# The kernel's last waits, for its stores, moved from SyncE to ScalarE and put in the order of the stores

## The chip, the cores and the metric

The kernel runs on one core of a Trainium2 chip. The metric is the device time of one execution in microseconds (us). The core has five instruction streams that run side by side and meet through semaphores: TensorE (PE, with its weight loads as PEld), VectorE (DVE), ScalarE (ACT), GpSimd (POOL) and SyncE (SP), which computes nothing here and issues transfers.

## The reference

```python
def setup_inputs():
    batch, seq, hidden, n_heads = (16, 512, 768, 12)
...
    y = np.matmul(x, weight)
    y = y.reshape(batch, seq, n_heads, head_dim)
    y1, y2 = (y[..., :head_dim // 2].copy(), y[..., head_dim // 2:].copy())
...
    out1 = y1 * cos1 - y2 * sin1
    out2 = y2 * cos2 + y1 * sin2
    out = np.concatenate([out1, out2], axis=-1)
    return out.reshape(batch, seq, hidden).astype(np.float32)
```

A projection of 16 x 512 rows by a 768 x 768 weight, and then the rotation of each of the 12 heads of 64 columns by cosines and sines that depend on the row. `x` and the result are float32, 25.17 MB each.

## The kernel before

The 8,192 rows are cut into 64 tiles of 128 rows, and four tiles make a group, so there are 16 groups; `LAST` is 15. A tile's rows are loaded as float32, cast to float16, turned so that the contracted dimension lies on the partitions, and multiplied by the weight into PSUM (`py`, in the last group also `pt`). VectorE multiplies PSUM by cosines and sines at once (line 412, into `tq`), and an addition, nearly always on GpSimd (line 429), puts the two products together into one of four output buffers `ov0` to `ov3`, each of which holds a group (128 x 3072 float32). `store` (line 453) issues a transfer of a part of such a buffer to the output, from the queue of the engine that is named to it: ScalarE (`"act"`) or SyncE (`"sp"`).

The order of the work is written out by hand. `Flow.do` records each instruction on its engine in the order of the calls and works out, from what was read and written before, which semaphores it waits for. Every store has a semaphore of its own, named for buffer and first column, `ov3_2560` for one; a store's landing adds 16 to it. Transfers are not ordered among themselves by anything else, so the program has to wait for the stores before it ends. `Flow.finish` (line 95) does that: it collects what wrote or read the named columns, drops what is already known to be past, and makes its engine wait for the rest. In this kernel thirteen semaphores remain: two for each of `ov0`, `ov1` and `ov2`, and seven for the pieces of the last group in `ov3`.

The last group's stores are issued in small pieces, since its sums come ready late: columns 0 to 768 from SyncE, 768 to 1536 from ScalarE, 1536 to 2048 from SyncE, 2048 to 2304 from ScalarE, 2304 to 2560 from SyncE, 2560 to 2816 from ScalarE and 2816 to 3072 from SyncE. The sum for the last of these is made by VectorE (`late`), those before it by GpSimd. `nc.gpsimd.drain()` at line 678 stands behind GpSimd's last addition.

In the built program, the waits of `finish` stand two to an instruction: six semaphore instructions on SyncE (line 102), and the thirteenth wait on the branch that leaves the kernel's body (line 116). The pairs, in the program's order, are 3_768 and 3_0, 3_1536 and 2_1536, 3_2048 and 2_0, 3_2304 and 1_1536, 3_2560 and 1_0, 3_2816 and 0_1536, and 0_0 on the branch. Then comes a closing sequence that the compiler adds. SyncE sets a semaphore, called the exit flag here. Each of the five engines has an instruction (a drain, on GpSimd a no-op) that waits for the exit flag and then reports. SyncE waits for the reports: one instruction for those of VectorE and TensorE, one for its own and ScalarE's, one for GpSimd's. After that, two barriers over all engines, with GpSimd in the middle and a clearing of semaphores between them, end the program (line 717).

Of the kernel before, what the change touches and what calls it, by code (L numbers as in the profile page):

```python
# [16 lines left out]
class Flow:  # L17
# [8 lines left out]
    def __init__(self, nc, tc):  # L26
        self.nc, self.tc = nc, tc
        self.eng = {
            "pe": nc.tensor, "dve": nc.vector, "act": nc.scalar,
            "pool": nc.gpsimd, "sp": nc.sync,  # L30
        }
        self.sems, self.count, self.known = {}, {}, {}
        self.wrote, self.readby = {}, {}
        self.seen = {e: {} for e in self.eng}

# [6 lines left out]
    def do(self, e, make, reads=(), writes=(), dma=None, tick=True, after=0):  # L42
        need = {}
        for k in reads:
            for s, v in self.wrote.get(k, {}).items():
                need[s] = max(need.get(s, 0), v)
        for k in writes:
            for d in (self.wrote, self.readby):
                for s, v in d.get(k, {}).items():
                    need[s] = max(need.get(s, 0), v)  # L50
        if e == "pe":
            need.pop("pe", None)
            if after:
                need["pe"] = after
        waits = self.settle(e, need)
        for s, v in waits[:-1]:
            self.eng[e].wait_ge(self.sem(s), v)
        i = make(self.eng[e])
        if waits:
            s, v = waits[-1]  # L60
            i.wait_op(self.sem(s), v, "sem-ge")
        name, step = (dma, 16) if dma else (e, 1)
        self.sem(name)
        at = self.count[name] + step
        if tick or dma:
            i.then_inc(self.sems[name], step)
            self.count[name] = at
            self.known[name, at] = dict(self.seen[e])
        for k in reads:
            d = self.readby.setdefault(k, {})  # L70
            d[name] = max(d.get(name, 0), at)
        for k in writes:
            self.wrote[k] = {name: at}
            self.readby[k] = {}
        return i
# [19 lines left out]
    def finish(self, e, keys):  # L95
        need = {}
        for k in keys:
            for d in (self.wrote, self.readby):
                for s, v in d.get(k, {}).items():
                    need[s] = max(need.get(s, 0), v)  # L100
        for s, v in self.settle(e, need):
            self.eng[e].wait_ge(self.sem(s), v)


# [1 line left out]
def kernel(  # L106
# [11 lines left out]
    f = Flow(nc, tc)  # L118
# [3 lines left out]
    B, S, H = x.shape  # L122
# [7 lines left out]
    QB = 4  # L130
# [3 lines left out]
    LAST = NG - 1  # L134
# [9 lines left out]
    NX, NB, NBH, NC, NCP, NXT, NXP, NOV = 10, 3, 3, 5, 2, 8, 4, 4  # L144
# [43 lines left out]
    def where(i):  # L188
        g, s = divmod(i, QB)
        return QB * (g // SB) + s, g % SB  # L190
# [10 lines left out]
    def load(i, e="sp"):  # L201
        b, r = where(i)
        k = ring("xs", NX)
        xs[i] = k
        do(e, lambda eng: eng.dma_start(  # L205
            out=xs_b[k], in_=x[b].rearrange("(p r) h -> r p h", r=SB)[r]),
            writes=[f"xs{k}"], dma=f"xs{k}")

    def load_quarter(gh, q):
        g, h = gh  # L210
        b, r = where(g * QB + 2 * h)
        e = BLOCKS[gh]
        src = x[b : b + 2].rearrange("b (j a r) (q k) -> r q a (b j) k", r=SB, a=R, q=NQ)
        if q == 0:
            xs[gh] = ring("xh", NBH) if e == "pool" else ring("xb", NB)
        k = xs[gh]
        name = f"xh{k}" if e == "pool" else f"xb{k}"
        buf = xh_b[k] if e == "pool" else xb_b[k]
        dst = buf.rearrange("p (j k) -> p j k", j=2 * NQ)
        do(e, lambda eng: eng.dma_start(out=dst[ts(q, R)], in_=src[r, q]),  # L220
           writes=[f"{name}q{q}"], dma=name)
# [3 lines left out]
    def load_w(c, e="sp"):  # L225
        t, h = c
        do(e, lambda eng: eng.dma_start(out=w_raw[:, t, h], in_=wv[t, h]),  # L227
           writes=[f"wr{t}{h}"], dma=f"w{t}{h}")
# [214 lines left out]
    def store(g, c0, c1, e):  # L443

        o = ov_of[g]
        b, r = where(g * QB)
        s0, s1 = c0 // H, -(-c1 // H)
        dst = out.rearrange("b (p r) h -> r p b h", r=SB)[r, :, b + s0 : b + s1]
        src = ov_b[o].rearrange("p (b h) -> p b h", b=QB)[:, s0:s1]
        if (c1 - c0) % H:  # L450
            dst = dst[:, 0, c0 - s0 * H : c1 - s0 * H]
            src = src[:, 0, c0 - s0 * H : c1 - s0 * H]
        do(e, lambda eng: eng.dma_start(out=dst, in_=src),
           reads=[f"ov{o}c{c}" for c in range(c0, c1, 64)], dma=f"ov{o}_{c0}")
# [153 lines left out]
    for g in range(LAST):  # L608
        for h in (0, 2):
            i = QB * (g + 1) + h  # L610
            q = (g, h * H, (h + 2) * H, "act")
# [6 lines left out]
            else:  # L618
                q = q[:3] + ("sp",)
# [22 lines left out]
    for i in range(QB, NTILE):  # L642
        g, s = divmod(i, QB)
# [35 lines left out]
    store(LAST, 2 * H, 2048, "sp")  # L679
    store(LAST, 2048, 3 * H, "act")  # L680
    store(LAST, 3 * H, 3 * H + 256, "sp")
    store(LAST, 3 * H + 256, 3 * H + 512, "act")
    for add in late:
        add()
    store(LAST, 3 * H + 512, 4 * H, "sp")
    f.finish("sp", [f"ov{o}c{c}" for o in range(NOV) for c in range(0, QB * H, 64)])


# [33 lines left out]
```

## Time and profile before

| | us |
|---|---|
| time before, median of 3 runs | 151.16 |
| the three runs | 151.91, 151.16, 151.03 |
| the profiled execution, its own time | 151.57 |
| its span, first to last instruction | 149.8 |
| lies around the span | 1.8 |
| PE busy | 141.1 (94%) |
| DVE busy | 126.4 (84%) |
| POOL busy | 122.9 (82%) |
| ACT busy | 78.0 (52%) |

TensorE is busy nearly throughout, until the last slices, in which the work runs off through VectorE, GpSimd and the stores. The mean granted TensorE clock is 0.989 of full speed. Starts are counted from the first instruction of the span. The views of the profile round starts to 0.1 us; where a text gives a start to the nanosecond, it is the start of the same record in the trace.

### The profile page before, as it was taken

To read this page: it belongs to the slowest core of one execution; us is meant where nothing else is said; L and a number is where in the kernel's file an instruction comes from. 1 tells how busy PE (TensorE), PEld (TensorE's weight loads), DVE (VectorE), ACT (ScalarE), POOL (GpSimd) and SP (SyncE) were. 2 spreads that over 40 slices of the span, in tenths; PEclk is the share of its full clock that TensorE was granted. 3 is DMA by queue.
4 is the path that set the end of the run, shared out by engine and by line. 5 is a ranking of instruction groups with operands and counts; after the bars stand their busy time and mean duration, and the time that the engine had idled before them with its cause. 6 is when DMAs were issued, how large, how long until landed. Compare 5 with 4: busy or idle time off the path is not lost.

```text
span 149.8 us, 4360 instructions
## 1 busy us (share of the span) xinstructions
PE 141.1 (94%) x1926; PEld 112.4 (75%) x1926; DVE 126.4 (84%) x92; ACT 78.0 (52%) x92; POOL 122.9 (82%) x68
## 2 busy tenths in 40 slices
PE   6969999999999999999999999999999999999940
PEld 2435578888888888888888888888888888856520
DVE  0154999887888899899999998999989998999980
ACT  3444798787777934456262905283336826163000
POOL 1000396999989998999999999999995979999990
PEclk9999999999999999999999999999999999999995
DMA  4999999999999999999999999999999999966683
GB/s 113 382 376 402 405 400 396 306 405 264 295 371 343 343 355 360 298 402 328 356 345 391 361 334 357 363 392 319 357 363 410 415 404 402 388 272 231 263 315 108
DMA packets 27555, 51.27 MB, mean 342 GB/s; under 512 B 7184, under 2 KB 13072, under 8 KB 27536
## 3 DMA queue, kind: packets, MB, share of 16 engines
q1 hardware_dynamic: 14592, 27.92, 53.9%
q10 hardware_dynamic: 7504, 21.10, 35.6%
q0 software_dynamic: 5440, 1.97, 10.7%
q8 instruction: 15, 0.25, 0.6%
q14 instruction: 4, 0.03, 0.1%
HBM read 27.79 MB, written 25.17 MB: 354 GB/s over the span
## 4 chain that ended last, share of the span: by engine, by line
PE 80%; DVE 6%; DMA 5%; POOL 3%; issue 2%; SPq 1%; POOLq 0%
PE py L360 70%; DMA w_raw<-in_weight_dram 5%; PE py L335 4%; PE pt L266 4%; POOL ov L429 3%; DVE w_raw L412 2%; DVE tq L412 2%; SPq L205 1%; PE pt L251 1%; DVE ov L429 1%; SPq L227 1%; POOLq L678 0%; DVE w_sb L185 0%; SPq L717 0%; SPq L116 0%
## 5 line engine op out<-in xcount | busy, mean ns | idle before, releaser
L429 POOL TENSOR_TENSOR ov<-tq 128x1536 f32<-128x1536 f32 (+3 forms) x31 | 77.5, 2520 | 19.4 <-DVE tq L412 19.3
L360 PE MATMUL py<-w_sb,xt 64*128 64x512 f16 (+1 forms) x864 | 81.4, 323 | 0.0
L412 DVE TENSOR_TENSOR tq<-py,csn 128x1024 f32<-128x1024 f32 (+2 forms) x46 | 74.6, 1652 | 5.2 <-PE py L360 4.9
L360 PEld LDWEIGHTS py<-w_sb,xt 64*128 64x128 f16 x864 | 61.0, 94 | 10.1 <-DVE tq L412 0.4
L185 ACT COPY xt<-pt 128x768 f16<-128x768 f16 x42 | 33.5, 800 | 45.7 <-PE pt L266 44.5
L185 ACT CAST xc<-xs 128x768 f16<-128x768 f32 x44 | 39.1, 907 | 13.9 <-DMA xs<-in_x_dram 13.7
L360 PE MATMUL py<-w_sb,xp 64*128 64x512 f16 (+1 forms) x432 | 42.6, 323 | 0.0
L412 DVE TENSOR_TENSOR w_raw<-py,csn 128x1024 f32<-128x1024 f32 (+1 forms) x21 | 35.2, 1674 | 3.7 <-PE py L360 3.5
L429 POOL TENSOR_TENSOR ov<-w_raw 128x1536 f32<-128x1536 f32 (+1 forms) x11 | 33.7, 3070 | 3.2 <-DVE w_raw L412 2.9
L360 PEld LDWEIGHTS py<-w_sb,xp 64*128 64x128 f16 x432 | 31.1, 94 | 4.7
L335 PE MATMUL py<-w_sb,xt 128*128 128x256 f16 (+1 forms) x90 | 15.7, 323 | 1.3 <-DVE w_sb L185 1.1
L266 PEld LDWEIGHTS pt<-ident,xc 64*128 64x128 f16 x456 | 14.8, 95 | 1.7 <-ACT xc L185 0.6
L266 PE MATMUL pt<-ident,xc 64*128 64x64 f16 x456 | 15.0, 190 | 0.0
L335 PEld LDWEIGHTS py<-w_sb,xt 128*128 128x128 f16 x90 | 8.1, 98 | 7.0 <-DVE w_sb L185 2.7
L220 POOL DMA_DIRECT2D xh<-in_x_dram x20 | 11.7, 590 | 0.0
L185 ACT CAST xd<-xb 128x1536 f16<-128x1536 f32 x5 | 8.2, 1636 | 0.2 <-DMA xb<-in_x_dram 0.2
L514 PE MATMUL py<-cold 128*128 128x512 f16 x12 | 5.0, 584 | 1.4 <-DVE cold L457 1.4
L185 DVE CAST w_sb<-w_raw 128x768 f16<-128x768 f32 x6 | 3.3, 558 | 3.4 <-DMA w_raw<-in_weight_dram 3.4
L294 DVE STREAM_TRANSPOSE xp<-xh 128x768 f32<-128x768 f32 x5 | 6.2, 1231 | 0.0
L185 DVE COPY xt<-pt 128x768 f16<-128x768 f16 x2 | 1.1, 558 | 5.5 <-PE pt L251 5.5
L294 DVE STREAM_TRANSPOSE xp<-xd 128x768 f32<-128x768 f32 x5 | 4.8, 969 | 0.0
L335 PE MATMUL py<-w_sb,xp 128*128 128x512 f16 (+1 forms) x24 | 4.2, 327 | 0.0
(20 smaller groups left out, 18.0 us busy)
## 6 DMA issues: line engine op xcount, KB each, us to landing
out_dram<-ov ACTq DMA_DIRECT2D x26, 768.0 KB, 8.6
xs<-in_x_dram SPq DMA_DIRECT2D x44, 384.0 KB, 17.7
xb<-in_x_dram SPq DMA_DIRECT2D x20, 192.0 KB, 17.4
out_dram<-ov SPq DMA_DIRECT2D x4, 768.0 KB, 4.7
w_raw<-in_weight_dram SPq DMA_DIRECT2D x6, 384.0 KB, 7.3
xh<-in_x_dram POOLq DMA_DIRECT2D x20, 96.0 KB, 12.9
out_dram<-ov SPq DMA_DIRECT2D x1, 384.0 KB, 2.6
out_dram<-ov ACTq DMA_DIRECT2D x1, 384.0 KB, 2.3
```

The costliest lines, as they stand in the source:

```text
L185: eng.copy(out=o, in_=i_) if e == "act" else eng.tensor_copy(out=o, in_=i_)
L205: do(e, lambda eng: eng.dma_start(out=xs_b[k], in_=x[b].rearrange("(p r) h -> r p h", r=SB)[r]), writes=[f"xs{k}"], dma=f"xs{k}")
L220: do(e, lambda eng: eng.dma_start(out=dst[ts(q, R)], in_=src[r, q]), writes=[f"{name}q{q}"], dma=name)
L227: do(e, lambda eng: eng.dma_start(out=w_raw[:, t, h], in_=wv[t, h]), writes=[f"wr{t}{h}"], dma=f"w{t}{h}")
L251: do("pe", lambda eng: eng.transpose(pt[:, t, h, :], src[:, t, h, :], ident), reads=[f"xc{c}", "ident"], writes=[f"pt{k}"], tick=(t, h) == ...
L266: do("pe", lambda eng: eng.transpose(pts[r][:, t, h, :], src[rows, t, h, :], ident[rows, rows]), reads=[f"xc{c}", "ident"], writes=[f"pt{r ...
L294: do("dve", lambda eng: eng.transpose(out=dst, in_=src), reads=rd, writes=[f"xp{z}"])
L335: do("pe", lambda eng: eng.matmul(ps, get(t, h), w_sb[:, t, h, a - s * H : z - s * H], start=start, stop=stop), reads=[key, f"w{t}{h}"], w ...
L360: do("pe", lambda eng: eng.matmul(py[:, a:z], get(t, h)[rows], w_sb[rows, t, h, a - s * H : z - s * H], start=start, stop=not opens and en ...
L412: do("dve", lambda eng: eng.tensor_tensor(out=tq.rearrange("p j (h d) -> p j h d", d=D), in0=ps.rearrange("p (h d) -> p h d", d=D) .unsque ...
L429: do(adder, lambda eng: eng.tensor_tensor(out=ov_b[o][:, ds(c0, w)].rearrange("p (h t d) -> p h t d", t=2, d=HD), in0=tq[:, 0].rearrange(" ...
L514: do("pe", lambda eng: eng.matmul(py[:, ts(b, 512)], cold[:, 0:P], cold, start=True, stop=warmed[0] < WARM - 6), reads=["cold"], writes=[f ...
```

## The change

`finish` is called for ScalarE in place of SyncE. Its waits are reduced to those for the stores' semaphores (names that begin with `ov`), sorted by the time at which they were last used, newest first, and handed out in a zigzag. `do` keeps, for each semaphore, a number that grows with every use, to sort by. The call that issues ScalarE's last store, of columns 2560 to 2816, is moved down behind SyncE's last one; each engine's own order of stores stays what it was.

```diff
-        self.sems, self.count, self.known = {}, {}, {}
+        self.sems, self.count, self.known, self.order = {}, {}, {}, {}
...
         self.sem(name)
+        self.order[name] = len(self.order) + sum(self.count.values())
         at = self.count[name] + step
...
-        for s, v in self.settle(e, need):
+        need = {s: v for s, v in need.items() if s.startswith("ov")}
+        old = sorted(self.settle(e, need), key=lambda q: -self.order[q[0]])
+        for s, v in old[:1] + old[1::2] + old[2::2][::-1]:
             self.eng[e].wait_ge(self.sem(s), v)
...
     store(LAST, 3 * H, 3 * H + 256, "sp")
-    store(LAST, 3 * H + 256, 3 * H + 512, "act")
     for add in late:
         add()
     store(LAST, 3 * H + 512, 4 * H, "sp")
-    f.finish("sp", [f"ov{o}c{c}" for o in range(NOV) for c in range(0, QB * H, 64)])
+    store(LAST, 3 * H + 256, 3 * H + 512, "act")
+    f.finish("act", [f"ov{o}c{c}" for o in range(NOV) for c in range(0, QB * H, 64)])
```

In the built program, the zigzag comes out as pairs from the oldest store to the newest: 0_0 and 0_1536, 1_0 and 1_1536, 2_0 and 2_1536, 3_0 and 3_768, 3_1536 and 3_2048, 3_2304 and 3_2816, all on ScalarE, and 3_2560 on ScalarE's branch. SyncE's branch waits for nothing. The closing sequence is the same, instruction for instruction: SyncE sets the exit flag, every engine reports behind it, and SyncE gathers the reports. On PE, DVE and POOL the program is unchanged apart from line numbers, and so is everything ahead of the last waits on SP and ACT.

## The prediction

> **What bounds the kernel now.** I read the chain of waits first. Most of it is matmul, which this change leaves as it is, so only its end matters. Asked for the stretch from 140 us on, in order of time (start, length, what), it closes like this:
>
> ```profile
> 142.80 1.96 POOL ov L429 x2
> 144.76 0.68 POOLq L678
> 145.44 0.86 POOL ov L429
> ```
>
> The last computing instruction, GpSimd's sum for columns 2560 to 2816, ends at 145.44 + 0.86 = 146.30 us. The span ends at 149.8, so 3.5 us lie behind it, and only there can the edit act. Next I read the transfers issued between 146.2 and 146.9 us and SyncE's waits from 146 us on (total, times, longest):
>
> ```profile
> out_dram<-ov ACTq DMA_DIRECT2D x1, 128.0 KB, 1.8
> ```
>
> ```profile
> SPq L102 <- DMA out_dram<-ov: 1.5, 2, 0.9
> ```
>
> ScalarE's last store is issued at 146.337 and needs 1.8 us to land; SyncE stands in line 102 for it, 0.9 us in the longest wait. The trace has the last update of that store's semaphore at 148.113, and the last of SyncE's own last store (columns 2816 on) at 147.762: ScalarE's is the store that ends last. So from 148.113 on, what counts is how many steps lie between this landing and the end. For these I read the instructions of line 102 and of line 116, engine by engine (count, durations in ns, first and last start):
>
> ```profile
> L102 SPq EVENT_SEMAPHORE  x6: 28/28/28, 146.4 to 148.2; - x6
> ```
>
> ```profile
> L116 SPq EVENT_SEMAPHORE  x3: 17/27/28, 148.4 to 148.7; - x3
> L116 SPq COMPARE_BRANCH  x1: 38/38/38, 148.3 to 148.3; - x1
> L116 ACTq DRAIN  x1: 8/8/8, 148.5 to 148.5; - x1
> L116 POOLq NOP  x1: 13/13/13, 148.5 to 148.5; - x1
> L116 DVEq DRAIN  x1: 17/17/17, 148.5 to 148.5; - x1
> L116 PEldq DRAIN  x1: 8/8/8, 148.5 to 148.5; - x1
> L116 SPq DRAIN  x1: 7/7/7, 148.5 to 148.5; - x1
> L116 SPq NOP  x1: 18/18/18, 148.7 to 148.7; - x1
> ```
>
> The reader is to see a string of short steps one behind the other. To the nanosecond, by the same records: landing 148.113; SyncE's wait for 2560 starts at 148.130, the next pair at 148.189, the branch at 148.257, the exit flag at 148.422. The four other engines report at 148.460 to 148.467, SyncE itself at 148.513. SyncE takes the reports of VectorE and TensorE at 148.592, its own and ScalarE's at 148.652, GpSimd's at 148.718. The two barriers then run to 149.79.
>
> **The change, part by part.** *The store call moved down.* Each engine issues the same stores in the same order with the same waits, so both last issues stay at 145.843 (SyncE) and 146.337 (ScalarE). Cost nothing; no queue is passed.
>
> *The waits taken from SyncE.* After its last store, which occupies it from 145.843 for 490 ns, SyncE goes on at once. The first thing behind it is now the exit flag: 146.33 plus one step of about 60 ns, near 146.4 where it was 148.422. SyncE's own report and its collection of VectorE's and TensorE's (done at 145.72 and before) then lie under the 1.8 us of the store. That takes off the path, after the landing, the pair with 2816 (59 ns, 148.130 to 148.189), the exit flag, all that hangs on it, and SyncE's first collection.
>
> *The waits put on ScalarE.* What is queued behind them on ScalarE is its report and the barriers alone; its last copy of data starts at 137.90 and takes 0.80. Six instructions start when its last store is issued, 146.337 + 0.339 = 146.68. SyncE's satisfied waits start 60 to 75 ns apart, so five of them are through by about 147.05: their newest semaphore, 2048, is full at 146.557. The sixth needs 2816, at 147.762. Then ScalarE reaches the branch, 0.35 us before 2560 lands. This is the cover for all six; if it were gone (2816 landing together with 2560) the sixth would add one step, 0.06 us.
>
> *The path after.* Landing 148.113, seen by the waiting branch some 20 ns later (SyncE's delay was 17): 148.13. From SyncE's branch to its next instruction took 148.422 − 148.257 = 0.165; I take the same for ScalarE's: its report starts at 148.30 and is set 17 ns later, at 148.315, as ScalarE's was (148.460 to 148.477). SyncE, waiting in the instruction for its own and ScalarE's reports, takes it some 20 ns later: 148.335. Before, that instruction started at 148.652. The rest, from there to the end, is unchanged. Gain: 148.652 − 148.335 = 0.317 us.
>
> The Trainium skill, "Runtime: NRT & Kernel Launch", section "Instruction fetch mechanics", says that a taken branch whose target is outside the fetched window must wait for its page to be read; the 0.165 us on SyncE's branch agrees with a target that was at hand, and by that row the sum stands, while by the rule ScalarE's branch, at another place of another stream, could stall as in the third rival.
>
> *The bounds.* The unseen operations are ScalarE's waiting branch and GpSimd's report without the flag to hold it. If ScalarE's branch cost only a plain step of 0.06 in place of 0.165, the gain would be 0.317 + 0.105 = 0.42. GpSimd's is bounded by this row of line 678:
>
> ```profile
> L678 POOLq DRAIN  x1: 3662/3662/3662, 144.4 to 144.4; - x1
> ```
>
> By it GpSimd's drain ends at 144.361 + 3.662 = 148.023, though its last addition ended at 146.30, and the report follows it. If that end holds, the report is set by about 148.09, 0.25 before it is asked for, and costs nothing. GpSimd was ready by 148.463 at the latest, as it answered the flag within 24 ns, and reported at 148.486. Were it ready only then, SyncE's no-op for GpSimd, which started at 148.718, would start at 148.507: gain 0.211. I take 0.317, since the drain's record is the nearer row, and keep 0.21 and 0.42 for the range. Below nothing only with a mechanism that the trace does not show, priced below.
>
> The sum against the profiled execution: 151.57 − 0.317 = 151.25, with the span at 149.79 − 0.32 = 149.47. That execution lies 0.41 above the median of the runs, in stretches that the edit does not touch, so the same gain is taken from the median: 151.16 − 0.32 = 150.84.
>
> **The rivals.** *No gain.* The moved waits were not what held the end: the store's landing shifts by as much as is saved, or GpSimd's leg is later than its records say (the profile calls its spans rough). For it: GpSimd's 1.7 us of drain after its last addition is unexplained. Against it: GpSimd answered within 24 ns of the flag, as the others did. Time: 151.16.
>
> *A larger gain.* If the two barriers also shortened because four engines now stand at the first one early, at most the 148.776 to 148.872 of SyncE's two drains and GpSimd's pick-up, 0.1, would go on top of 0.42: 0.5, or 150.65. Against it: SyncE still checks in last, in the same instructions.
>
> *Slower: ScalarE's branch waits for its instructions.* The place is the branch with the wait for 2560, which now lies on the path. The price is bounded by rows: the instruction queue's pages of 8 KB took 0.309 us of packet time each from 65 us on, the last at 139.25; a whole trip from issue to landing of a small transfer on an otherwise quiet queue took 1.78 (the last store). The point from which it decides is a stall of 0.317 us beyond the 0.165 already counted. So it ranges from 151.15 (0.309) to 152.62 (1.78), about 151.8 midway. For it: an added load of seven waits shifts ScalarE's stream. Against it: the stream runs straight on there, and SyncE's branch at the same place showed no such wait. By the skill's rule above it would come out so if the target's page were missing.
>
> *The change does nothing.* The zigzag could come out in the wrong order; the built program shows the pairs oldest first and 2560 on the branch, so this has no chance of its own.
>
> **How the numbers follow.** 0.74 for the forecast (150.84, by the bounds 150.74 to 150.95), 0.12 for no gain (151.16), 0.05 for the larger gain (150.65), 0.06 for the stall (151.15 to 152.62), 0.03 for a disturbance of more than 1% either way that no row names. The runs before reach from 0.13 below to 0.75 above their median, more than the whole effect, so the range takes this scatter about the forecast and no gain: 150.3 to 151.7, leaving out the upper part of the stall, the unnamed, and some scatter, together under 2 in 10. One per cent is 1.5 us, about what a measurement of this kernel can tell from no change; the forecast, no gain, the larger gain and the most of the stall lie inside it. Same 0.94, faster 0.03, slower 0.03, the slower from the top of the stall and a half of the unnamed.
>
> **What would show it.** Line 119's exit flag (line 116 before) near 146.4 in place of 148.4; no SyncE waits in the line of `finish`, and six on ScalarE from 146.7, the sixth ending near 147.8; ScalarE's branch starting within 0.03 us of the last update of 2560's semaphore, and its report 0.165 later; the end of the span 1.36 us after that landing in place of 149.787 − 148.113 = 1.67. The first step is wrong if 2816 lands after 2560 or the exit flag still comes late; the second if GpSimd's report is set after ScalarE's; the third if ScalarE's report is more than 0.3 us after the branch. Wrong altogether would be a span that differs by more than half a microsecond in work before 146 us, which nothing here accounts for.

## The result, and the profile after

The changed kernel takes 151.07 us, the median of 17 runs (150.36 to 153.43), beside 151.91 for the kernel before, also of 17 (151.03 to 153.23). The ratio is 0.9939, with a 95% interval of 0.9914 to 0.9965: 0.9 us faster, where the forecast had 0.3, and inside the one per cent that the forecast called the same. The ratio leaves out runs more than 1.5% above the fastest of their own kernel, which are three of the changed kernel (152.67, 152.68 and 153.43) and none of the kernel before; over all 17 runs of each the means are 151.31 and 151.88, a ratio of 0.996.

The profiled execution took 152.67 us, with a span of 150.89 and 1.78 around it, as before. That is 1.6 us above the median, so its span cannot be set against the 149.79 of before as a whole. Its end can. The chain of waits from 140 us on closes as before (start, length, what):

```profile
144.25 1.96 POOL ov L432 x2
146.21 0.68 POOLq L681
146.89 0.86 POOL ov L432
```

GpSimd's last addition ends at 147.755, ScalarE's last store is issued at 147.786 and lands at 149.565, 1.78 us later, as before (1.78). Now the instructions of the waits and of the closing sequence (count, durations in ns, first and last start), which were lines 102 and 116 before and are 105 and 119 now:

```profile
L105 ACTq EVENT_SEMAPHORE  x6: 38/38/576, 148.2 to 148.7; - x6
```

```profile
L119 SPq EVENT_SEMAPHORE  x3: 17/28/1661, 147.8 to 148.1; - x3
L119 DVEq DRAIN  x1: 17/17/17, 147.9 to 147.9; - x1
L119 PEldq DRAIN  x1: 8/8/8, 147.9 to 147.9; - x1
L119 SPq DRAIN  x1: 61/61/61, 147.9 to 147.9; - x1
L119 POOLq NOP  x1: 13/13/13, 149.5 to 149.5; - x1
L119 ACTq COMPARE_BRANCH  x1: 33/33/33, 149.6 to 149.6; - x1
L119 ACTq DRAIN  x1: 8/8/8, 149.7 to 149.7; - x1
L119 SPq NOP  x1: 18/18/18, 149.8 to 149.8; - x1
```

The reader is to see what has moved ahead of the landing. The exit flag (the first of SyncE's three) comes at 147.8, right behind the last store's issue, and VectorE, TensorE and SyncE report at 147.9, under the store. SyncE then sits for 1661 ns in the instruction that takes ScalarE's report. Behind the landing, ahead of the barriers, there are only ScalarE's branch at 149.586, its report at 149.741 and SyncE's no-op at 149.825. From the landing to the end of the span it is 150.893 − 149.565 = 1.328 us, and before it was 1.674: 0.346 us less. This stretch, from the last landing to the end of the span, is called the end below.

This span is 1.1 us longer all the same, and where that comes from is seen further up. In the kernel before, the chain from 96 to 120 us is TensorE's alone, of which this is one piece:

```profile
99.88 5.85 PE py L360 x54
```

In this execution it begins with a load:

```profile
77.47 23.34 DMA xb<-in_x_dram
...
100.83 0.39 ACT xd L188
101.22 1.12 issue
102.34 0.81 ACT xt L188
```

A load of `x` that was 23 us under way lets ScalarE cast late, and its copy of the turned tile comes late with it; by 116 us TensorE stands 1.46 us behind the same instructions of before, 0.23 of it since the first 20 us. ScalarE's waits for the other loads of `x` between 75 and 120 us (total, times, longest) also grew, first after, then before:

```profile
ACT xc L188 <- DMA xs<-in_x_dram: 15.4, 7, 4.3
```

```profile
ACT xc L185 <- DMA xs<-in_x_dram: 6.1, 3, 2.5
```

The program up to there is the same in both. Later profiles show the row both ways in either kernel: the changed one has it small in after_third, and the kernel before has it large in before_again:

```profile
ACT xc L188 <- DMA xs<-in_x_dram: 6.3, 3, 2.6
```

```profile
ACT xc L185 <- DMA xs<-in_x_dram: 16.8, 7, 4.4
```

So the late loads are not tied to the change.

### The profile page after: what moved, and what is told of

Same layout as the page of the kernel before. It is cut to its first block, busy times and chain, and to the rows that moved or that the text cites. A ratio compares the mean times of both kernels' runs of the same rounds, so it can differ in the third digit from the quotient of the medians.

```text
span 150.9 us, 4360 instructions
## 1 busy us (share of the span) xinstructions
PE 141.5 (94%) x1926; PEld 111.2 (74%) x1926; DVE 126.7 (84%) x92; ACT 78.0 (52%) x92; POOL 122.8 (81%) x68
## 4 chain that ended last, share of the span: by engine, by line
PE 61%; DMA 20%; DVE 6%; POOL 3%; issue 3%; ACT 2%; SPq 1%; POOLq 0%
PE py L363 52%; DMA xb<-in_x_dram 15%; DMA w_raw<-in_weight_dram 5%; PE py L338 4%; PE pt L269 4%; POOL ov L432 3%; DVE w_raw L415 2%; DVE tq L415 2%; ACT xt L188 1%; SPq L208 1%; PE pt L254 1%; DVE ov L432 1%; ACT xc L188 1%; SPq L230 1%; POOLq L681 0%
## 5 line engine op out<-in xcount | busy, mean ns | idle before, releaser
L363 PE MATMUL py<-w_sb,xt 64*128 64x256 f16 (+1 forms) x864 | 81.6, 323 | 0.3 <-ACT xt L188 0.3
```

Source lines behind the costliest of these rows:

```text
L363: do("pe", lambda eng: eng.matmul(py[:, a:z], get(t, h)[rows], w_sb[rows, t, h, a - s * H : z - s * H], start=start, stop=not opens and en ...
```

## The experiments

Two theories. T: the change acts only in the end, is worth 0.35 us, and the rest of the 0.9 is the scatter of the runs. R: it also saves some 0.5 us in another place. The end is read from each kernel's trace to the nanosecond; the time of the whole comes from 12 runs of each kernel beside 35 of the kernel before on the same chip, except for the first sample (17 of each) and the last two kernels (one run).

| kernel | last addition ends, us | end, us | median, us | before, us | ratio, 95% interval | ratio by T from the measured end |
|---|---|---|---|---|---|---|
| before | 146.31 | 1.674 | | | | |
| changed (first) | 147.76 | 1.328 | 151.07 | 151.91 | 0.9939 [0.9914, 0.9965] | 0.9977 |
| before_again | 148.86 | 1.677 | 151.61 | 151.74 | 1.0015 [0.9972, 1.0057] | 1.0000 |
| after_again | 149.06 | 1.328 | 152.08 | 151.74 | 0.9980 [0.9939, 1.0021] | 0.9977 |
| after_third | 146.14 | 1.327 | 151.45 | 151.84 | 0.9981 [0.9942, 1.0021] | 0.9977 |
| sp_sorted | 146.48 | 1.549 | 151.48 | 151.74 | 0.9987 [0.9948, 1.0025] | 0.9992 |
| act_unsorted | 147.61 | 1.482 | 152.08 | 151.84 | 1.0006 [0.9966, 1.0047] | 0.9987 |
| dve_sorted | 146.71 | 1.484 | 151.22 | 151.84 | 0.9971 [0.9939, 1.0003] | 0.9987 |
| act_drain | 145.51 | 1.220 | 151.19 | 151.84 | 0.9947 [0.9912, 0.9983] | 0.9970 |
| act_more | 145.59 | 2.867 | 152.72 | 151.74 | 1.0061 [1.0019, 1.0103] | 1.0079 |
| pool_late | 145.68 | 2.150 | 151.37 | 151.20 | one run | |
| pool_free | 148.24 | 1.333 | 153.16 | 151.20 | one run | |

The last column is 1 plus the difference of the end from 1.674, divided by the median of before. The ratios are formed as in the section on the result, so that of after_again can lie below 1 though its median is above.

**The two kernels once more** (before_again, after_again, after_third; no edit).

> The kernel before, against itself. Both theories expect a ratio of 1.000 and an end (last landing of the 2560 store to the end of the span) of 1.67 us. How far the ratio comes out from 1.000, and how wide its interval is, tells how much of the 0.6% measured for the change can be scatter of the runs. Theory T (the change acts only behind the last landing, and is worth 0.35 us or 0.23%; what is above that is scatter) expects that two such samples of one kernel can differ by some 0.3 to 0.4%. Theory R (the change also saves some 0.5 us elsewhere) expects 1.000 within 0.1%.

> The changed kernel once more, beside the kernel before on one chip. T expects a ratio of 0.9977 (151.9 less 0.35) and an end of 1.33 us. R expects 0.994 again.

> The changed kernel a third time, to tell 0.9977 (T) from 0.994 (R) with more runs. End 1.33 us by both.

The ends come out the same to 3 ns in all five profiles of the two kernels, while the last addition in front of them, at which all twelve profiles arrive by the same instructions, ends anywhere between 145.5 and 149.1 us. That time goes with the row of ScalarE's waits for `x` that the section on the result shows. In seven profiles the row is 1.8 to 6.8 us in total, and the last addition ends between 145.5 and 146.7. In the other five it is 15.4 to 18.3, the chain between 60 and 125 us runs through a load of `x`, and the last addition ends between 147.6 and 149.1. Both kernels stand in both groups. What makes the loads late is not shown.

The kernel before against itself came out 0.15% off, with an interval of 0.4% either way. The changed kernel gave 0.9980 and 0.9981, by T's number and not by R's, though the first interval still holds R's 0.994 and the second, from 0.9942, only just leaves it out. So three samples of one change read 0.9939, 0.9980 and 0.9981. Put together, weighted by the intervals and taken as independent, they give 0.9957 with an interval of 0.9938 to 0.9977, which has T's 0.9977 at its edge. Much hangs on which runs the ratio counts: from the means of all runs the same three samples give 0.9962, 1.0011 and 0.9965. Put together in the same way, with intervals from the scatter of the runs, they give 0.9972 with an interval of 0.9950 to 0.9995. T's 0.9977 lies near its middle and R's 0.994 outside.

**sp_sorted**: the changed kernel, with the waits in the stores' order, but on SyncE.

```diff
-    f.finish("act", [f"ov{o}c{c}" for o in range(NOV) for c in range(0, QB * H, 64)])
+    f.finish("sp", [f"ov{o}c{c}" for o in range(NOV) for c in range(0, QB * H, 64)])
```

> The waits in the order of the stores, but on SyncE: its branch waits for 2560 itself, and the exit flag comes after it as in the kernel before. The two steps between the wait for 2560 and the branch (148.130 to 148.257) are off the path: T expects an end of 1.674 - 0.127 = 1.55 us and a ratio of 0.9992. A variant of R in which the order of the waits gives the gain expects 0.994; one in which it is SyncE's freedom, 0.999 to 1.000.

The end is 1.549, as T expected (1.55). The closing sequence (as above):

```profile
L119 SPq EVENT_SEMAPHORE  x3: 17/28/28, 148.4 to 148.7; - x3
L119 SPq COMPARE_BRANCH  x1: 38/38/38, 148.3 to 148.3; - x1
```

The landing is at 148.258, the branch that waits for it at 148.275, and the exit flag only behind it, at 148.443: the order alone takes away the two steps between, 0.125 us, and leaves the flag and all that hangs on it behind the landing. The interval of the ratio, from 0.9948, leaves out the 0.994 that a gain by the order alone would have given.

**act_unsorted**: the kernel before, with its order, but with the waits on ScalarE.

```diff
-    f.finish("sp", [f"ov{o}c{c}" for o in range(NOV) for c in range(0, QB * H, 64)])
+    f.finish("act", [f"ov{o}c{c}" for o in range(NOV) for c in range(0, QB * H, 64)])
```

> The waits on ScalarE, but in the order of the kernel before, so that the pair with 2816 and the branch stand behind the wait for 2560. T: the engine alone is worth most of the gain, and the order the two steps behind 2560, 2 x 0.077 = 0.15 us on ScalarE: end 1.33 + 0.15 = 1.48 us, ratio 0.9987. A variant of R in which the engine gives 0.9 us expects 0.994.

The end is 1.482 (expected 1.48). The waits are line 102 here, the closing sequence line 116:

```profile
L102 ACTq EVENT_SEMAPHORE  x6: 38/38/38, 148.0 to 149.5; - x6
```

```profile
L116 ACTq COMPARE_BRANCH  x1: 33/33/33, 149.6 to 149.6; - x1
L116 ACTq DRAIN  x1: 8/8/8, 149.8 to 149.8; - x1
```

The landing is at 149.428; the wait for it starts at 149.449, the pair with 2816 at 149.526, the branch at 149.602. The engine alone is worth 1.674 − 1.482 = 0.192 us, and the order, on ScalarE, 1.482 − 1.328 = 0.154. The time of the whole shows no gain at all (1.0006), but its interval holds T's 0.9987 and not R's 0.994. That speaks against the engine as the source of what the first sample showed above 0.35.

**act_more**: 20 more wait instructions on ScalarE behind the landing.

```diff
         old = sorted(self.settle(e, need), key=lambda q: -self.order[q[0]])
+        old = old[:1] * 41 + old[1:]
```

> The changed kernel with 20 more wait instructions on ScalarE between the last landing and its branch, all for the semaphore that has just been filled, at 0.077 us a step: 1.54 us more behind the last landing. T expects an end of 1.33 + 1.54 = 2.87 us and, since nothing covers it, a time 1.54 above the changed kernel and 1.54 - 0.35 = 1.19 above the kernel before: ratio 1.0078. R, with 0.5 us saved elsewhere, expects some 0.7 us above the kernel before: 1.0045. If the end of the span were hidden behind something else, the time would rise by less than the end does.

The end is 2.867 (expected 2.87). Line 106 has the waits here, line 120 the closing sequence:

```profile
L106 ACTq EVENT_SEMAPHORE  x26: 38/38/560, 146.0 to 148.9; - x26
```

```profile
L120 ACTq COMPARE_BRANCH  x1: 38/38/38, 148.9 to 148.9; - x1
L120 ACTq DRAIN  x1: 8/8/8, 149.1 to 149.1; - x1
```

The landing is at 147.375; from the first of the twenty at 147.396 to the branch at 148.929 they stand 0.077 apart. The time rises with the end: 1.0061, and the interval, 1.0019 to 1.0103, does not hold 1. So the end is on the path, and nothing covers it. Between T's 1.0078 and R's 1.0045 this does not decide.

**act_drain**: a drain on ScalarE that takes over the branch's wait.

```diff
     f.finish("act", [f"ov{o}c{c}" for o in range(NOV) for c in range(0, QB * H, 64)])
+    nc.scalar.drain()
```

> The changed kernel with a drain on ScalarE that carries the wait for 2560, so that the branch waits for nothing, as the branches of the other engines. T: the step from the waiting branch to ScalarE's report, 0.155 us, becomes a plain step of 0.08: end 1.33 - 0.07 = 1.26 us, ratio 0.9972. If the drain has to wait for more of ScalarE than a branch does, the end stays at 1.33 or rises.

The end is 1.220, a little better than expected (1.26):

```profile
L690 ACTq DRAIN  x1: 8/8/8, 147.3 to 147.3; - x1
```

```profile
L119 ACTq DRAIN  x1: 8/8/8, 147.4 to 147.4; - x1
```

The branch no longer appears. The landing is at 147.316, the new drain at 147.337, the report at 147.384: 0.047 from one to the next, where from the waiting branch it was 0.155. That is the 0.108 by which this end is shorter than the changed kernel's. Of all kernels here this has the shortest end, 0.45 below the kernel before, and its ratio (0.9947, interval 0.9912 to 0.9983) is below 1; against the changed kernel the 0.11 us is shown in the trace alone, as it is below what the runs can tell.

**dve_sorted**: the changed kernel with all waits on VectorE (`f.finish("dve", ...)`).

> All thirteen waits on VectorE, in the order of the stores. Its report is taken one instruction earlier than ScalarE's. T: one step of SyncE more behind the report, 0.06 us: end 1.39 us, ratio 0.9981. A theory in which it matters that ScalarE waits for its own store expects an end nearer to 1.67.

The end is 1.484, not 1.39:

```profile
L119 SPq EVENT_SEMAPHORE  x3: 17/28/28, 146.8 to 148.9; - x3
L119 DVEq COMPARE_BRANCH  x1: 47/47/47, 148.5 to 148.5; - x1
L119 DVEq DRAIN  x1: 17/17/17, 148.7 to 148.7; - x1
L119 SPq NOP  x1: 18/18/18, 148.9 to 148.9; - x1
```

Two terms were too small. VectorE needs 0.200 from its branch (148.543) to its report (148.743), ScalarE 0.155. And SyncE, which takes VectorE's report first, has two steps before its no-op (148.786, 148.861, 148.932), where behind ScalarE's report it has one that it is already waiting in: 0.189 from the report's start to the no-op against 0.084. Together that is 0.15 of the 0.156 by which the end is longer. So an engine that did not issue the last store can hold the waits too, and better than SyncE in the order of before. Of the two terms, the larger (0.105 against 0.045) is at which step SyncE takes the report.

**pool_late** and **pool_free**: GpSimd's report later, and GpSimd without its drain.

```diff
     nc.gpsimd.drain()
+    for _ in range(21):
+        nc.gpsimd.wait_ge(f.sem("pe"), 1)
```

```diff
-    nc.gpsimd.drain()
```

> The changed kernel with 21 waits on GpSimd, for a semaphore that is long past, behind its drain: ten instructions at some 0.075 us and a waiting branch of 0.165, so that its report comes some 0.9 us later than in the changed kernel, where it was set 0.22 before ScalarE's. Theory T with GpSimd's records as they are: once the 0.22 us and the 0.05 that SyncE's instruction for ScalarE covers are used up, the rest comes on top: end 1.33 + 0.65 = 1.98 us (1.9 to 2.05). If GpSimd were ready much earlier than its drain's record says, the end would be nearer to 1.33; if it were later, above 2.05.

> The changed kernel without the drain on GpSimd behind its last addition. T: GpSimd's leg is covered, so the end stays at 1.33 us, and only GpSimd's report comes earlier, or the same time is spent in its next drain. If the drain had held back the end or the last store, the end or the store's landing would come sooner: an end below 1.30, or less than 1.74 us from issue to landing.

With the late report the end is 2.150, above the 1.9 to 2.05 that was expected:

```profile
L683 POOLq EVENT_SEMAPHORE  x10: 42/43/43, 147.4 to 148.2; - x10
```

```profile
L119 POOLq COMPARE_BRANCH  x1: 42/42/42, 148.3 to 148.3; - x1
L119 POOLq NOP  x1: 13/13/13, 148.5 to 148.5; - x1
```

GpSimd's drain ends at 147.400 by its record, and the first wait starts at 147.449, right behind it: GpSimd is indeed held until then. The excess lies in the steps: ten of 0.087 where 0.075 was taken, and 0.178 behind the branch where it was 0.165, 0.13 in all. The rest, 0.04, is that the drain ended 0.05 before the landing here and 0.09 before it in the changed kernel's first profile. SyncE's no-op at 148.534 follows GpSimd's report at once: GpSimd's leg is now the end.

Without the drain the end is 1.333 and the store needs 1.78 us, as T expected. These rows are GpSimd's report and its drains in the final barriers:

```profile
L119 POOLq NOP  x1: 13/13/13, 148.4 to 148.4; - x1
```

```profile
L720 POOLq DRAIN  x3: 45/137/1692, 148.4 to 151.1; - x3
```

The report, at 148.359, comes 0.12 us after the last addition, where it was 1.76, and the next drain behind it takes 1.692 us in place of 47 ns: the time is spent one instruction later. That drain ends at 150.134, which is 0.085 behind the landing at 150.049 but ahead of ScalarE's report at 150.225, so it costs nothing here.

## Why the prediction was right, and where its size was off

**What bounds the end.** Right: in every profile the store of 2560 lands last, 0.34 to 0.37 us after SyncE's, and act_more shows that a step behind this landing costs its full length.

**The store call moved down** cost nothing: SyncE's last store is issued at 147.297 and ScalarE's at 147.786, 0.489 apart, as before (0.494).

**SyncE set free.** Right: the exit flag comes 0.054 behind the issue of the last store instead of 0.309 behind its landing. The forecast put it at 146.4 in a run in which that store is issued at 146.34.

**The waits on ScalarE are covered.** Right: the first starts 0.379 after the last issue, the fifth 0.690 after it, and the sixth ends 0.325 before 2560 lands.

**The path after.** Forecast 0.317, measured 0.346, inside the bounds of 0.211 and 0.42. The 0.029 between them is two terms: the branch takes 0.155 on ScalarE, not SyncE's 0.165; and the 0.02 for SyncE to notice the report had been counted ahead of a full step of 0.066, while the no-op starts 0.067 after the report's update, 0.02 included. The 0.42 assumed a branch at the price of a plain step; act_drain, which has a plain step there, gives 1.674 − 1.220 = 0.45.

**GpSimd's leg.** Right: its report is set at 149.540, 0.218 before ScalarE's (148.315 − 148.09 = 0.225 by the forecast's figures), and pool_late shows what it costs when that cover is gone.

**The stall of ScalarE's branch**, the rival on the slower side, did not come: 0.155 to 0.156 from the branch to the report in three profiles of the changed kernel, where the Trainium skill's rule ("Runtime: NRT & Kernel Launch", "Instruction fetch mechanics") would have it wait for a page if the target's were missing. In the first of these profiles the last page of the instruction queues is through at 141.37, ahead of this branch at 149.586, so no page was read for it; what a missing page costs, no run here shows. The larger gain through shorter barriers did not come either: from SyncE's no-op to the end it is 1.068 us after and 1.069 before.

**The size of the whole.** The forecast was 150.84 and the first sample gave 151.07, but beside a kernel before at 151.91, so the drop was 0.84 where 0.32 had been worked out. That the time came so close is luck in part: the median that the forecast started from was 0.75 below that of the 17 runs, and taken from 151.91 the same gain would have given 151.59. The step that was too small is the one on scatter: the prediction took 0.13 below to 0.75 above the median from three runs, and the runs of the kernel before alone go from 150.59 to 154.34. The median of one repeat of the changed kernel, 152.08, lies outside the range of 150.3 to 151.7, beside a kernel before at 151.74. The ratios of the repeats came out at the size of the end, 0.2%. The one per cent that the forecast took for what a measurement can tell was too wide: the kernel before against itself has an interval of 0.4% either way. Whether the changed kernel gains something more ahead of the last addition stays open: the three samples together leave room for 0.2 to 0.6% by their ratios, and for 0.05 to 0.5% by the means of all runs. If it does, it is not around the span (1.77 to 1.86 us in all profiles) and not in the end, and the trace offers no place for it, since the instructions up to the last stores are the same; but the spread of the last addition's time, 3.5 us over all profiles and 1.2 us over the seven without the late loads, is too wide to rule it out.

**The sign of being wrong altogether** came: the work ahead of the last addition took 1.45 us longer in the changed kernel's first profile, where more than half a microsecond was to count against the forecast. It does not: the late loads of `x` go with it, and they come in either kernel. But the forecast had no term for them, though the profiles with and without them differ by more than the change is worth.

Two small sums of the forecast are off and move nothing: midway between 151.15 and 152.62 lies 151.9, not 151.8, and half of the unnamed 0.03 is 0.015, not the 0.03 given to faster.

## What to carry to other kernels

Behind the last transfer, count the steps from its landing to the end, and let each of them that does not need the landing stand before it: wait in the order in which the stores land, on an engine whose report is taken late, and not on the engine that has to announce the exit to the others. Such an edit is worth a few tenths of a microsecond, shows to the nanosecond in the trace, and is lost in the runs' scatter here. Before reading a ratio of half a per cent, run the kernel before against itself.

## What the runs showed of the hardware

A drain on GpSimd behind an addition takes 1.7 us, counted from the end of the addition or from its own start, whichever comes later. In the changed kernel it is issued before the last addition begins and ends 1.718 after that addition; in all eleven profiles that have it, it is 1.717 to 1.719:

```profile
L681 POOLq DRAIN  x1: 3664/3664/3664, 145.8 to 145.8; - x1
```

In pool_free the first drain starts 0.203 after the addition's end and lasts 1.692. GpSimd's other drains in the final barriers take 0.04 to 0.14.

A satisfied wait costs a step of 0.06 to 0.075 us on SyncE, 0.077 to 0.081 on ScalarE and 0.087 on GpSimd. A branch that waits costs 0.155 to 0.161 on ScalarE, 0.165 to 0.168 on SyncE, 0.178 on GpSimd (one profile) and 0.200 on VectorE (one profile) until the next instruction starts. One that waits for nothing leaves no record and little time, as act_drain shows with 0.047.

In these records, an instruction with two waits starts when the first is satisfied, and its duration holds the wait for the second. ScalarE's sixth in the changed kernel starts 0.021 after 2304's landing at 148.643 and ends 0.027 after 2816's at 149.213, which makes the 576 ns of its row. A long duration on such a row is waiting, and a short one does not say that there was no wait before it.
